# RWKV block inverse in 64x64 quarters of TensorE, interleaved pairs and heads, gated rows on two engines, and the block loop in another place

## The chip, the cores and the metric

The kernel runs on one core of one Trainium2 chip. The metric is the device time of one execution, in microseconds (us), as the median of several runs. A core has TensorE (PE; its weight loads are shown apart as PEld), VectorE (DVE), ScalarE (ACT), GpSimd (POOL) and SyncE (SP), which here only issues transfers; every engine works through its own instructions in order, and semaphores make one wait for another. DMA queues move data between the chip's large memory and the on-chip memory.

## What is computed

One decoder layer over 256 tokens of width 2048, in float32. The input is normalised and projected; 8 attention heads of 128 and 16 RWKV heads of 64 work on the projections beside each other; their outputs are projected back and added to the input. Then comes PEER, a retrieval over 128 x 128 experts of one neuron each, and a last normalisation.

```python
def rwkv7_time_mix(...):
    def step(state, inp):
        rt, wt, kt, vt, at, bt = inp
        sa = jnp.einsum('bhij,bhj->bhi', state, at)
        state = (state * wt[:, :, None, :] + sa[..., None] * bt[:, :, None, :]
                 + vt[..., :, None] * kt[..., None, :])
        y = jnp.einsum('bhij,bhj->bhi', state, rt)
        return state, y
...
def peer_ffn(x, wq, sub_keys, u, v):
    q = (xt @ wq).reshape(T, H, 2, PEER_HALF)
    s = jnp.einsum('thpc,hpnc->thpn', q, sub_keys).astype(jnp.float32)
    sv, si = lax.top_k(s, K)
    cand = (sv[:, :, 0, :, None] + sv[:, :, 1, None, :]).reshape(T, H, K * K)
    best, bi = lax.top_k(cand, K)
    ...
    expert = (i1 * PEER_NKEYS + i2).astype(jnp.int32)
    gates = jax.nn.softmax(best, axis=-1)
    def chunk(args):
        hpre = jnp.einsum('cd,chkd->chk', xc, u[ec]).astype(jnp.float32)
        act = (jax.nn.gelu(hpre, approximate=False) * gc).astype(x.dtype)
        return jnp.einsum('chk,chkd->cd', act, v[ec])
...
h = h + jnp.concatenate([attn, rw], axis=-1) @ w_out[l]
h = h + peer_ffn(rmsnorm(h, norm2_g[l]), peer_wq[l], peer_sub_keys[l], peer_u[l], peer_v[l])
return rmsnorm(h, final_g)
```

## The kernel before

Products of float32 precision are made of three passes: weights and inputs are split into a rounded high part and the rest (`whi`, `wlo`). `prefetch` (L191) loads half a block of weights by SP's queue, ACT writes `whi` (L204), DVE writes `wlo` (L205), and `gemm_half` (L213) multiplies (L218 to L220). The order in which weights are fetched is the list `halves`, which must be the order in which the loops consume them.

**Stage A, 0 to 541 us: input projections, RWKV and attention.** `products` (L639) runs the gemms of 8 RWKV pairs (two heads of 64 in the 128 rows) and then of 8 attention heads. After each pair or head a generator, `rwkv` (L376) or `attn` (L578), joins the list `live`; `step_all` advances up to four of them by one step between parts of gemms. In these generators the sequence is cut in NC = 4 chunks of CH = 64 tokens. A chunk needs the inverse of a triangular 64x64 matrix per head. It is built by doubling in five levels: `X` is the transpose of `XT` (L493), one group of four matmuls (one per chunk) gives `pw` (L496), DVE masks it into `wm` (L498), a second group gives `px` (L502), which DVE adds to `XT` (L504). Both heads of a pair stand in one 128x128 block-diagonal matrix, so that each matmul has 128 rows and 128 weight columns and 64 moving columns. The inverse is applied to a 128-wide right side after that. `clear` (L633) issues transfers that set the expert table `rows_d` in memory to zero, two for each pair and one for each head.

**541 to 736 us**: the output projection and PEER's queries.

**Stage D, 736 to 1568 us: the hidden stage.** `hidden` (L1125) goes over the 128 keys of u. A key takes 16 matmuls of 512 columns by `whi` (L240) and 16 of 256 by `wlo` (L242), from two halves of u, so two `wlo` splits of DVE. Then ACT and DVE sum the two parts (`part`, L1137 and L1138; the key's partial sum), and ACT writes the gelu into `A` (L1122), a ring of tiles of eight keys. Beside the keys three generators run, paced by shares of PE's time (`beside`): `both_choices` finds each token's experts (DVE), `tables` makes the table of gates by expert (DVE and POOL; marks, L937 and L939), then `places`, the row of each expert in a packed table; and `scatter` (L1098) takes a key's gelu, multiplies it by its gates into `at` (`gated`, L1080, the multiplication is L1093) and writes the rows of that key to their places in `rows_d` by an indirect DMA that POOL issues (L1107). `at` is a tile of seven keys' rows; the first key of a tile also copies the expert numbers into its last columns (`eint`, L1085). `gates_of` (L1072) loads the gates of eight keys. All of it is on POOL for the first 126 keys. The scheduler sets the place of each instruction on its engine from this program order and from its own estimate of when operands are ready.

**Stage E, 1568 to 2029 us: the values.** Blocks of 128 packed experts are read back, their rows of v gathered and multiplied into 8 accumulators (two token halves t, four columns each). Two lists of 28 blocks belong to one half only; 52 blocks are for both. A loop `For_i(MID, count)` behind them takes what stands beyond 52; `count` is computed, and here it is not above 52, so the loop makes no trip.

**Tail**: DVE adds the residual to the eight accumulators (`yr`, L1295), then the last norm and the output.

Of the kernel before, what the change touches and what calls it, by code (L numbers as in the profile page):

```python
# [10 lines left out]
F32 = mybir.dt.float32  # L11
# [57 lines left out]
def consts():  # L69
# [6 lines left out]
    c[:, K_MSK:K_MSK + P] = same & (p[:, None] < p[None])  # L76
# [3 lines left out]
    for i in range(6):  # L80
        n = 1 << i
        lv = (p[:, None] // (2 * n) == p[None] // (2 * n)) & (p[:, None] % (2 * n) >= n) & (p[None] % (2 * n) < n)
        c[:, K_LV + i * P:K_LV + (i + 1) * P] = lv
        if i == 0:
            c[:, K_M1T:K_M1T + P] = lv.T
# [69 lines left out]
def block_kernel(ctx: ExitStack, tc: tile.TileContext, x, cols, consts, w_lora, w_gate, w_rkv, w_qkv,  # L155
# [25 lines left out]
    for w, n in ((w_gate, 2), (w_rkv, 3 * RJ), (w_qkv, 3 * AH)):  # L181
        halves += [(w[m, i].rearrange("p k c -> p (k c)"), HK * P) for m in range(n) for i in range(2)]
# [163 lines left out]
    wms = [p1.tile([P, NC, P], F32, name=f"wm{i}") for i in range(1, 6)]  # L346
# [8 lines left out]
    mska = kc(K_MSK, 128).rearrange("p (h t) -> p h t", h=2).unsqueeze(1).to_broadcast([P, 2, 2, CH])  # L355
    mskr = kc(K_MSK + 128, 192).unsqueeze(1).to_broadcast([P, 2, 192])
# [3 lines left out]
    idb = ident.unsqueeze(1).to_broadcast([P, NC, 128])  # L360
# [15 lines left out]
    def rwkv(j, r, k, vv):  # L376
# [94 lines left out]
        XT = W("XT", [P, NC, 128], 2)  # L471
        lv = lambda i: kc(K_LV + i * 128, 128)
        nc.vector.tensor_tensor(XT, M[:, :, 0:128], kc(K_M1T, 128).unsqueeze(1).to_broadcast([P, NC, 128]),
# [10 lines left out]
        for i in range(1, 6):  # L484
            n = 1 << i
            nblk = P // (2 * n)
# [13 lines left out]
            px = bank("px", [P, NC, CH])  # L500
# [138 lines left out]
    def products():  # L639
# [18 lines left out]
        for j in range(RJ):  # L658
            while len(live) > 4:
                step_all()  # L660
# [13 lines left out]
        for h in range(AH):  # L674
            while len(live) > 4:
                step_all()
# [646 lines left out]
```

## Time and profile before

| | |
|---|---|
| median of 3 runs | 2046.03 us (2045.47 to 2049.38) |
| profiled execution | 2048.21 us, its span 2046.3 us |
| PE busy | 1935.7 us (95%) |
| DVE busy | 1437.7 us (70%) |
| ACT busy | 1062.9 us (52%) |
| POOL busy | 712.1 us (35%) |
| hidden stage | 736 to 1568 us of the span |
| value stage | 1600 to 2029 us, PE busy throughout |

The profile is one execution. A window of it gives how long each engine was busy in a stretch, the granted TensorE clock as a share of full speed, and what the DMA engines moved. A wait is put down to the instruction that came last. Where a mean of a line mixes shapes, the single rows are read.

### The profile page before, as it was taken

To read this page: it belongs to the slowest core of one execution; us is meant where nothing else is said; L and a number is where in the kernel's file an instruction comes from. 1 tells how busy PE (TensorE), PEld (TensorE's weight loads), DVE (VectorE), ACT (ScalarE), POOL (GpSimd) and SP (SyncE) were. 2 spreads that over 40 slices of the span, in tenths; PEclk is the share of its full clock that TensorE was granted. 3 is DMA by queue.
4 is the path that set the end of the run, shared out by engine and by line. 5 is a ranking of instruction groups with operands and counts; after the bars stand their busy time and mean duration, and the time that the engine had idled before them with its cause. 6 is when DMAs were issued, how large, how long until landed. Compare 5 with 4: busy or idle time off the path is not lost. (4 is left out here: it accounts for less than half of the span.)

```text
span 2046.3 us, 31447 instructions
## 1 busy us (share of the span) xinstructions
PE 1935.7 (95%) x11804; PEld 1723.3 (84%) x11804; DVE 1437.7 (70%) x2090; ACT 1062.9 (52%) x1696; POOL 712.1 (35%) x654
## 2 busy tenths in 40 slices
PE   7888999999999999999999999887998999999996
PEld 6788999999879998878888888776887788888885
DVE  6766878766556888999878866544755666666665
ACT  4534554345455444677676744433444555555554
POOL 7211211100000000023424269998986333333322
PEclk9999999999999999999999999998999999999998
DMA  8999322225576666556666678786888887878783
GB/s 248 258 247 246 98 87 87 88 83 146 190 227 198 184 180 188 173 175 197 215 195 217 196 237 264 248 267 229 270 267 271 343 284 280 296 286 293 281 297 141
DMA packets 135291, 443.91 MB, mean 217 GB/s; under 512 B 14369, under 2 KB 52257, under 8 KB 118497
## 3 DMA queue, kind: packets, MB, share of 16 engines
q1 hardware_dynamic: 106992, 289.24, 47.7%
q0 software_dynamic: 28144, 152.65, 20.4%
q8 instruction: 93, 1.52, 0.3%
q14 instruction: 62, 0.50, 0.1%
HBM read 380.07 MB, written 61.76 MB: 216 GB/s over the span
## 5 line engine op out<-in xcount | busy, mean ns | idle before, releaser
L205 DVE TENSOR_TENSOR wlo<-raw,whi 128x1024 fp32r<-128x1024 f32 (+1 forms) x408 | 569.6, 1402 | 301.1 <-ACT whi L204 291.9
L240 PE MATMUL ps_gm<-nx,whi 128*128 128x512 f32 x2048 | 731.8, 400 | 24.9 <-ACT whi L204 21.9
L204 ACT ACTIVATE whi<-raw 128x1024 fp32r<-128x1024 f32 (+1 forms) x408 | 429.5, 1055 | 384.2 <-issue 89.5
L242 PE MATMUL ps_gm<-nx,wlo 128*128 128x256 f32 x2048 | 579.4, 283 | 14.2 <-DVE wlo L205 14.2
L240 PEld LDWEIGHTS ps_gm<-nx,whi 128*128 128x128 f32 x2048 | 387.8, 189 | 112.6 <-ACT whi L204 22.6
L242 PEld LDWEIGHTS ps_gm<-nx,wlo 128*128 128x128 f32 x2048 | 390.3, 191 | 20.1 <-DVE wlo L205 19.7
L249 DVE TENSOR_TENSOR vlo<-vraw,vhi 128x2048 fp32r<-128x2048 f32 x108 | 247.9, 2297 | 151.6 <-ACT vhi L248 146.1
L248 ACT ACTIVATE vhi<-vraw 128x2048 fp32r<-128x2048 f32 x108 | 205.9, 1913 | 156.3 <-DVE vlo L249 146.8
L1205 POOL DMA_INDIRECT vraw<-in_v_dram,ag x108 | 145.1, 1343 | 294.8 <-PE ps_gm L1194 210.0
L218 PE MATMUL ps_gm<-xh,whi 128*128 128x256 f32 x640 | 192.7, 301 | 0.8 <-ACT whi L204 0.8
L220 PE MATMUL ps_gm<-xh,wlo 128*128 128x256 f32 x640 | 185.1, 289 | 3.2 <-DVE wlo L205 3.1
L219 PE MATMUL ps_gm<-xl,whi 128*128 128x256 f32 x640 | 185.6, 290 | 0.0
L1107 POOL DMA_INDIRECT rows_d<-at,place x126 | 169.5, 1345 | 36.9 <-POOL at L1093 15.8
L951 POOL TENSOR_TENSOR mt<-gc 128x1024 f32<-128x1024 f32 x16 | 39.7, 2482 | 345.5 <-ACT gc L979 345.5
L1122 ACT ACTIVATE A<-part 128x256 f32<-128x256 f32 x128 | 53.1, 415 | 166.7 <-DVE part L1138 131.3
L1093 POOL TENSOR_TENSOR at<-A,gt 128x256 f32<-128x256 f32 x126 | 129.2, 1041 | 5.4 <-DMA gt<-gate_d 3.6
L220 PEld LDWEIGHTS ps_gm<-xh,wlo 128*128 128x128 f32 x640 | 122.8, 192 | 4.6 <-DVE wlo L205 4.2
L218 PEld LDWEIGHTS ps_gm<-xh,whi 128*128 128x128 f32 x640 | 122.9, 192 | 1.9 <-ACT whi L204 1.2
L219 PEld LDWEIGHTS ps_gm<-xl,whi 128*128 128x128 f32 x640 | 122.9, 192 | 0.7
L807 POOL DMA_DIRECT2D skb<-in_sk_dram x16 | 8.6, 540 | 250.7 <-ACT mh L248 167.7
L945 ACT ACTIVATE ob<-ob,pick 128x128 f32<-128x128 f32 x256 | 83.9, 390 | 19.6 <-DVE ob L937 19.6
L373 POOL TENSOR_TENSOR df<-ext 128x256 f32<-128x256 f32 (+1 forms) x28 | 23.8, 850 | 155.3 <-DVE ext L371 142.4
(1521 smaller groups left out, 3925.5 us busy)
## 6 DMA issues: line engine op xcount, KB each, us to landing
raw<-in_u_dram SPq DMA_DIRECT2D x256, 512.0 KB, 4.1
raw<-in_w_rkv_dram SPq DMA_DIRECT2D x48, 512.0 KB, 7.3
raw<-in_w_qkv_dram SPq DMA_DIRECT2D x48, 512.0 KB, 3.6
rows_d<-zt SPq DMA_DIRECT2D x23, 1028.0 KB, 15.8
raw<-in_w_out_dram SPq DMA_DIRECT2D x32, 512.0 KB, 3.9
raw<-in_wq_dram SPq DMA_DIRECT2D x32, 512.0 KB, 3.6
gate_d<-gc SPq DMA_DIRECT2D x16, 1024.0 KB, 6.5
gt<-gate_d POOLq DMA_DIRECT2D x16, 1024.0 KB, 9.0
```

The lines of the kernel that those rows point to most:

```text
L204: nc.scalar.activation(hi[:, :n], raw[:, :n], AF.Copy)
L205: state["dve"] = nc.vector.tensor_tensor(lo[:, :n], raw[:, :n], hi[:, :n].bitcast(F32), op=ALU.subtract)
L218: nc.tensor.matmul(ps, a, xh(kt), start=first and k == 0, stop=False)
L219: nc.tensor.matmul(ps, a, xl(kt), start=False, stop=False)
L220: state["mm"] = nc.tensor.matmul(ps, b, xh(kt), start=False, stop=last and k == HK - 1)
L240: nc.tensor.matmul(ps.rearrange("p z t -> p (z t)"), hi[:, k * P:(k + 1) * P], x_.rearrange("p z t -> p (z t)"), start=i + k == 0, stop=Fa ...
L242: state["mm"] = nc.tensor.matmul(ps[:, 0, :], lo[:, k * P:(k + 1) * P], x_[:, 0, :], start=False, stop=i == 1 and k == HK - 1, skip_group_ ...
L248: nc.scalar.activation(hi, src, AF.Copy)
L249: nc.vector.tensor_tensor(lo, src, hi.bitcast(F32), op=ALU.subtract)
L1093: eng.tensor_tensor(at[:, 0:T].rearrange("p (q t) -> p q t", q=KT), As[i2 // 8][:, k, :].rearrange("p (q t) -> p q t", q=KT), g.rearrange( ...
L1107: s_ = nc.gpsimd.indirect_dma_start(out=rows_d, out_offset=bass.IndirectOffsetOnAxis(ap=place[:, i2:i2 + 1], axis=0), in_=at, in_offset=None)
L1205: nc.gpsimd.indirect_dma_start(out=raw, out_offset=None, in_=vf, in_offset=bass.IndirectOffsetOnAxis(ap=ag[:, T:ROW].bitcast(I32), axis=0))
```

## The change

*Compact inverse.* `XT`, `X` and the `wm` tiles hold only the two 64x64 diagonal blocks, one above the other, [P, NC, 64] instead of [P, NC, 128]. Each level's group of four matmuls of 128x128 weights and 64 moving columns becomes eight matmuls, each on one head: 64 rows, 64 weight columns, 32 moving columns, rows and outputs in the same half of the partitions. The two mask operations behind `pc` become one. After the last level the compact inverse is expanded to its block-diagonal form by one POOL operation (`bd(XB_, XT)`).

*Order.* RWKV pairs and attention heads alternate: pairs 0, 1, 2, head 0, pair 3, head 1, up to pair 7, head 5, head 6, head 7. The weight list follows. After the first head the splits use one pool of tiles, as they did before after the last pair.

*Hidden stage.* `tables` waits until both halves are chosen. Shares and paces of the generators change. The multiplication of a gated row is on VectorE for even keys and on POOL for odd ones; the copy of the expert numbers stays on POOL.

*The block loop* stands in the middle of the value stage (at k == 40), not behind it.

```diff
+    ORDER = [("r", 0), ("r", 1)] + [x for j in range(2, RJ) for x in (("r", j), ("a", j - 2))] + [("a", AH - 2), ("a", AH - 1)]
+    blocks_ = [(w_gate, m) for m in range(2)]
+    for what, n in ORDER:
+        blocks_ += [((w_rkv if what == "r" else w_qkv), 3 * n + i) for i in range(3)]
...
-    wms = [p1.tile([P, NC, P], F32, name=f"wm{i}") for i in range(1, 6)]
+    wms = [p1.tile([P, NC, CH], F32, name=f"wm{i}") for i in range(1, 6)]
...
+    both = [slice(0, 64), slice(64, 128)]
...
-            nc.vector.tensor_tensor(M[:, q:q + 2, 0:128].rearrange("p a (h t) -> p a h t", h=2),
-                                    pc2[:, :, 0:CH].unsqueeze(2).to_broadcast([P, 2, 2, CH]), mska, op=ALU.mult)
-            nc.vector.tensor_tensor(M[:, q:q + 2, 128:320], pc2[:, :, CH:], mskr, op=ALU.mult)
+            nc.vector.tensor_tensor(M[:, q:q + 2, 64:320], pc2, msk, op=ALU.mult)
...
-            X = W("X", [P, NC, 128], XB)
+            X = W("X", [P, NC, CH], XB)
             nc.vector.transpose(X.rearrange("p c s -> p (c s)"), XT.rearrange("p c s -> p (c s)"))
-            pw = bank("pw", [P, NC, CH])
+
+            pw = bank("pw", [P, NC, CH // 2])
             for c in range(NC):
-                nc.tensor.matmul(o4(pw)[:, c], M[:, c, 0:128], lo_(X)[:, c], start=(c == 0), stop=(c == NC - 1),
-                                 skip_group_check=True)
+                for hs in both:
+                    nc.tensor.matmul(o4(pw)[hs, c], M[hs, c, 64:128], lo_(X)[hs, c], start=True, stop=True,
+                                     skip_group_check=True)
...
-                nc.tensor.matmul(o4(px)[:, c], wm[:, c, :], hi_(XT)[:, c], start=(c == 0), stop=(c == NC - 1),
-                                 skip_group_check=True)
+                for hs in both:
+                    nc.tensor.matmul(o4(px)[hs, c], wm[hs, c, :], hi_(XT)[hs, c], start=True, stop=True,
+                                     skip_group_check=True)
...
+        XB_ = W("XB", [P, NC, 128], 2)
+        bd(XB_, XT)
...
-            nc.tensor.matmul(sa_p, XT[:, c, :], r0, start=True, stop=True)
+            nc.tensor.matmul(sa_p, XB_[:, c, :], r0, start=True, stop=True)
...
+        for k, (what, n) in enumerate(ORDER):
+            while len(live) > 4:
+                step_all()
+            if what == "a":
+                state["pools"] = [spl]
+            yield from (pair if what == "r" else head)(n)
...
-        while t not in chosen:
+        while 0 not in chosen or 1 not in chosen:
             yield 0
...
-            yield 1.5
+            yield 2.6
...
-            eng.tensor_copy(rows[0][:, 0:n * ROW].rearrange("p (n c) -> p n c", c=ROW)[:, :, T].bitcast(I32),
+            nc.gpsimd.tensor_copy(rows[0][:, 0:n * ROW].rearrange("p (n c) -> p n c", c=ROW)[:, :, T].bitcast(I32),
                                   eint[:, i2:i2 + n])
...
-            at = gated(i2)
+            at = gated(i2, nc.gpsimd if i2 % 2 else nc.vector)
...
-            yield 1.5
+            yield 2.3
...
-    beside = [[both_choices(), 0.55, 0.0], [tables(), 0.38, 0.0], [scatter(), 1.0, 0.0]]
+    beside = [[both_choices(), 0.6, 0.0], [tables(), 0.45, 0.0], [scatter(), 1.0, 0.0]]
...
+        if k == 40:
+
+            count = nc.values_load(nblk[0:1, 0:1], min_val=0, max_val=128,
+                                   skip_runtime_bounds_check_because="a count of at most 16384 experts in blocks of 128")
+            with tc.For_i(MID, count, 1) as i:
+                rows[2] = rows[1]
+                ag, _ = rows_at(i * P + BM)
+                rows[1] = rows[2]
+                block((0, 1), *divided(ag, gather(ag)), False)
```

How this moves instructions, at two places. Numbers behind a name tell buffers apart; `xN` is a run of alike instructions.

VectorE in the hidden stage, around the 82nd key, before: two splits of u and one partial sum for each key, and nothing else.

```order
L1138 TENSOR_TENSOR part_13604<-part_13604,ps_gm_13548 128x256
L205 TENSOR_TENSOR wlo_13670<-raw_13667,whi_13669 128x1024
L205 TENSOR_TENSOR wlo_13699<-raw_13696,whi_13698 128x1024
L1138 TENSOR_TENSOR part_13663<-part_13663,ps_gm_13607 128x256
L205 TENSOR_TENSOR wlo_13729<-raw_13726,whi_13728 128x1024
L205 TENSOR_TENSOR wlo_13756<-raw_13753,whi_13755 128x1024
L1138 TENSOR_TENSOR part_13722<-part_13722,ps_gm_13666 128x256
```

VectorE around the 82nd key now (L211 is the split, L1151 the partial sum, L1106 the multiplication of a gated row; `at_13919` holds the rows of keys 21 to 27, `at_14065` those of 28 to 34, `at_14222` the next seven):

```order
L1151 TENSOR_TENSOR part_13847<-part_13847,ps_gm_13793 128x256
L1106 TENSOR_TENSOR at_13919<-A2_9503,gt0_13651 128x256
L1106 TENSOR_TENSOR at_13919<-A3_9958,gt1_13833 128x256 x2
L211 TENSOR_TENSOR wlo_13907<-raw_13904,whi_13906 128x1024
L1106 TENSOR_TENSOR at_14065<-A3_9958,gt1_13833 128x256
L211 TENSOR_TENSOR wlo_13934<-raw_13931,whi_13933 128x1024
L1151 TENSOR_TENSOR part_13900<-part_13900,ps_gm_13850 128x256
...
L1106 TENSOR_TENSOR at_14065<-A4_10422,gt0_14000 128x256 x2
L211 TENSOR_TENSOR wlo_13989<-raw_13986,whi_13988 128x1024
L1151 TENSOR_TENSOR part_13957<-part_13957,ps_gm_13903 128x256
...
L1106 TENSOR_TENSOR at_14222<-A4_10422,gt0_14000 128x256 x2
```

The gated rows of even keys from 22 on stand among the splits of some three keys; the rows of keys 0 to 20 stand at keys 75 to 77, and none between.

POOL in its scatters before (L1093 the multiplication, L1107 the scatter, L1085 the copy of expert numbers, L1075 the load of gates): two rows are made, then two are scattered.

```order
L1093 TENSOR_TENSOR at_13247<-A2_9154,gt0_13178 128x256 x2
L1107 DMA rows_d_70<-at_13247,place_8196 39936x257 x2
L1085 COPY at_13355<-eint_8197 128x7
L1093 TENSOR_TENSOR at_13355<-A2_9154,gt0_13178 128x256 x2
L1107 DMA rows_d_70<-at_13355,place_8196 39936x257 x2
```

POOL in its scatters now (L1106, L1120, L1098 and L1088 are the same four), from the end of the tile `at_13761` of keys 14 to 20:

```order
L1106 TENSOR_TENSOR at_13761<-A2_9503,gt0_13651 128x256
L1120 DMA rows_d_70<-at_13761,place_8536 39936x257 x2
L1098 COPY at_13919<-eint_8537 128x7
L1106 TENSOR_TENSOR at_13919<-A2_9503,gt0_13651 128x256 x2
L1120 DMA rows_d_70<-at_13919,place_8536 39936x257 x4
L1088 DMA gt0_14000<-gate_d_69 128x16x128
L1106 TENSOR_TENSOR at_13919<-A3_9958,gt1_13833 128x256
L1120 DMA rows_d_70<-at_13919,place_8536 39936x257 x2
L1106 TENSOR_TENSOR at_13919<-A3_9958,gt1_13833 128x256
L1098 COPY at_14065<-eint_8537 128x7
```

One row is made for two scatters, and the copy into a new tile stands where it stood, behind the scatters of the tile before it; VectorE's rows of that tile wait for this copy.

## Rows read from the trace of the kernel before

**Rows 1.** The page: busy time, share of the span and instructions of each engine.

```profile
PE 1935.7 (95%) x11804; PEld 1723.3 (84%) x11804; DVE 1437.7 (70%) x2090; ACT 1062.9 (52%) x1696; POOL 712.1 (35%) x654
```

**Rows 2.** Windows: stretch, length, busy of each engine, granted clock, DMA share, GB/s.

```profile
100.00:150.00 50.00, 44.25 (x351) 43.62 (x350) 33.14 (x68) 21.14 (x34) 8.71 (x15) 0.93 1.07 251
200.00:541.00 341.00, 336.06 (x2702) 326.18 (x2701) 249.73 (x495) 159.64 (x302) 37.26 (x46) 1.00 0.35 104
...
1219.83:1568.20 348.37, 317.44 (x1770) 273.85 (x1768) 201.68 (x168) 147.95 (x221) 310.95 (x276) 0.96 0.79 256
...
2029.00:2046.00 17.00, 0.19 (x1) 0.00 (x0) 10.62 (x20) 8.42 (x22) 6.06 (x4) 0.61 0.33 124
```

**Rows 3.** Windows of line L1138 (partial sums) alone: DVE busy, clock, DMA.

```profile
736.00:1219.83 483.83, 29.52 (x72) 0.99 0.64 198
749.80:788.60 38.80, 2.90 (x7) 1.00 0.65 190
```

**Rows 4.** Waits from 1220 to 1568 us, and windows of all engines around one.

```profile
ACT A L1122 <- POOL at L1093: 30.7, 2, 21.8
PE ps_gm L240 <- ACT whi L204: 21.9, 2, 17.0
...
1370.00:1392.00 22.00, 4.97 (x29) 4.16 (x27) 0.80 (x3) 1.70 (x3) 19.64 (x23) 0.67 0.46 155
1392.00:1420.00 28.00, 27.54 (x144) 23.57 (x144) 16.31 (x15) 12.06 (x20) 23.94 (x23) 0.89 0.82 269
```

**Rows 5.** Lines L496 and L218 by form, L496's window after 200 us, and timeline.

```profile
L496 PEld LDWEIGHTS ps_pw<-X,M x320: 186/192/192, 96.7 to 431.3; 128*128 128x128 f32 x160
L218 PEld LDWEIGHTS ps_px<-xh,ml x8: 160/162/165, 13.5 to 16.9; 128*96 128x96 f32 x8
200.00:541.00 341.00, 30.84 (x240) 29.58 (x240) 1.00 0.35 104
232.33 0.97 PEld L496 LDWEIGHTS ps_pw<-X,M 128*128 128x128 f32 x8 [0.22 <-issue]
```

**Rows 6.** Line L493 on VectorE: times in ns, least, median, most.

```profile
L493 DVE STREAM_TRANSPOSE X<-XT x40: 685/702/714, 95.6 to 429.8; 128x512 f32<-128x512 f32 x40
```

**Rows 7.** POOL's timeline from 1235 us: start, length, instruction, idle before; and L1107.

```profile
1235.63 1.20 POOL L1075 DMA_DIRECT2D gt<-gate_d  x1
...
1241.99 0.96 POOL L1107 DMA_INDIRECT rows_d<-at,place  x1 [0.30 <-issue]
1242.97 1.81 POOL L1093 TENSOR_TENSOR at<-A,gt 128x256 f32<-128x256 f32 x2
1244.95 1.81 POOL L1107 DMA_INDIRECT rows_d<-at,place  x1 [0.16 <-POOL at L1093]
...
1249.80 0.21 POOL L1085 COPY at<-eint 128x7 int32<-128x7 int32 x1
...
L1107 POOL DMA_INDIRECT rows_d<-at,place x126: 961/1054/2045, 1219.8 to 1563.4; - x126
```

**Rows 8.** POOL's timeline from 1381 us, while the other engines stand still.

```profile
1381.02 1.66 POOL L1093 TENSOR_TENSOR at<-A,gt 128x256 f32<-128x256 f32 x2
1382.84 1.01 POOL L1107 DMA_INDIRECT rows_d<-at,place  x1 [0.17 <-POOL at L1093]
1384.15 0.97 POOL L1107 DMA_INDIRECT rows_d<-at,place  x1 [0.30 <-issue]
```

**Rows 9.** Window of all engines while the experts are chosen.

```profile
900.00:940.00 40.00, 33.87 (x210) 29.66 (x209) 40.00 (x45) 25.37 (x52) 16.56 (x10) 1.00 0.51 167
```

**Rows 10.** Timeline of the tail: the first final sum, and the seventh.

```profile
2029.58 0.69 DVE L1295 TENSOR_TENSOR yr<-yr,ps_mm 128x512 f32<-128x512 f32 x1 [7.86 <-PEq L1264]
...
2034.63 0.66 DVE L1295 TENSOR_TENSOR yr<-yr,ps_gm 128x512 f32<-128x512 f32 x1
```

**Rows 11.** POOL's timeline: the first and the seventh scatter, and what follows.

```profile
1219.83 2.04 POOL L1107 DMA_INDIRECT rows_d<-at,place  x1 [5.86 <-DVE place L1060]
...
1230.13 0.22 POOL L1085 COPY at<-eint 128x7 int32<-128x7 int32 x1
```

More of the change, by code (lines that the diff above doesn't have):

```diff
@@ L75, in consts @@
     same = p[:, None] // 64 == p[None] // 64
-    c[:, K_MSK:K_MSK + P] = same & (p[:, None] < p[None])
+    c[:, K_MSK + 64:K_MSK + P] = (p[:, None] % 64) < np.arange(64)[None]
     c[:, K_MSK + P:K_MSK + 192] = (p[:, None] % 64) <= np.arange(64)[None]
@@ L81, in consts @@
         n = 1 << i
-        lv = (p[:, None] // (2 * n) == p[None] // (2 * n)) & (p[:, None] % (2 * n) >= n) & (p[None] % (2 * n) < n)
-        c[:, K_LV + i * P:K_LV + (i + 1) * P] = lv
+        r, t = p[:, None] % 64, np.arange(64)[None]
+        lv = lambda a, b: (a // (2 * n) == b // (2 * n)) & (a % (2 * n) >= n) & (b % (2 * n) < n)
+        c[:, K_LV + i * 64:K_LV + (i + 1) * 64] = lv(r, t)
         if i == 0:
-            c[:, K_M1T:K_M1T + P] = lv.T
+            c[:, K_M1T:K_M1T + 64] = lv(t, r)
+            c[:, K_M1T + 64:K_M1T + 128] = r == t
     c[:, K_HM:K_HM + P] = (p[:, None] // 64 == np.arange(P)[None] // 64)
@@ L180, in block_kernel @@
         halves += [(w_lora[m, i].rearrange("p k c -> p (k c)"), HK * LOR) for m in range(2)]
-    for w, n in ((w_gate, 2), (w_rkv, 3 * RJ), (w_qkv, 3 * AH)):
-        halves += [(w[m, i].rearrange("p k c -> p (k c)"), HK * P) for m in range(n) for i in range(2)]
+    ORDER = [("r", 0), ("r", 1)] + [x for j in range(2, RJ) for x in (("r", j), ("a", j - 2))] + [("a", AH - 2), ("a", AH - 1)]
+    blocks_ = [(w_gate, m) for m in range(2)]
+    for what, n in ORDER:
+        blocks_ += [((w_rkv if what == "r" else w_qkv), 3 * n + i) for i in range(3)]
+    halves += [(w[m, i].rearrange("p k c -> p (k c)"), HK * P) for w, m in blocks_ for i in range(2)]
     KP = (4, 5, 6, 7, 0, 1, 2, 3)
@@ L359, in block_kernel @@
     hm2 = lambda t: t.unsqueeze(1).to_broadcast([P, 2, CH])
-    idb = ident.unsqueeze(1).to_broadcast([P, NC, 128])
+    idb = kc(K_M1T + 64, 64).unsqueeze(1).to_broadcast([P, NC, CH])
+    both = [slice(0, 64), slice(64, 128)]
     def bd(dst, src):
@@ L465, in rwkv @@
             pc2 = pc.rearrange("p (c i) n -> p c (i n)", c=2)
-            nc.vector.tensor_tensor(M[:, q:q + 2, 0:128].rearrange("p a (h t) -> p a h t", h=2),
-                                    pc2[:, :, 0:CH].unsqueeze(2).to_broadcast([P, 2, 2, CH]), mska, op=ALU.mult)
-            nc.vector.tensor_tensor(M[:, q:q + 2, 128:320], pc2[:, :, CH:], mskr, op=ALU.mult)
+            nc.vector.tensor_tensor(M[:, q:q + 2, 64:320], pc2, msk, op=ALU.mult)
             yield
-        XT = W("XT", [P, NC, 128], 2)
-        lv = lambda i: kc(K_LV + i * 128, 128)
-        nc.vector.tensor_tensor(XT, M[:, :, 0:128], kc(K_M1T, 128).unsqueeze(1).to_broadcast([P, NC, 128]),
+        XT = W("XT", [P, NC, CH], 2)
+        lv = lambda i: kc(K_LV + i * 64, 64)
+        nc.vector.tensor_tensor(XT, M[:, :, 64:128], kc(K_M1T, 64).unsqueeze(1).to_broadcast([P, NC, CH]),
                                 op=ALU.mult)
@@ L485, in rwkv @@
             n = 1 << i
-            nblk = P // (2 * n)
+            nblk = CH // (2 * n)
             lo_ = lambda t: t.rearrange("p c (b z i) -> p c b z i", z=2, i=n)[:, :, :, 0, :]
@@ L657, in products, with pair @@
         state["pools"] = [spl, spl, spare[0]]
-        for j in range(RJ):
-            while len(live) > 4:
-                step_all()
+        def pair(j):
             got = []
@@ L672, in products, with head @@
             clear(2)
-        state["pools"] = [spl]
-        for h in range(AH):
-            while len(live) > 4:
-                step_all()
+        def head(h):
             got = []
@@ L1260, in block_kernel @@
                 block((t,), *cut[j], ends[t] == j)
-    count = nc.values_load(nblk[0:1, 0:1], min_val=0, max_val=128,
-                           skip_runtime_bounds_check_because="a count of at most 16384 experts in blocks of 128")
-    with tc.For_i(MID, count, 1) as i:
-        ag, _ = rows_at(i * P + BM)
-        block((0, 1), *divided(ag, gather(ag)), True)
+        if k == 40:
[6 more added lines that the diff above has]
+                block((0, 1), *divided(ag, gather(ag)), False)
     gf = mp.tile([P, D], F32, tag="ml", name="gf")
```

5 lines of the change are left out of this document (2 added, 3 removed).

## The prediction

> **What bounds the kernel now.** The profiled execution took 2048.2 us, 2.2 us above the median of the runs; its span is 2046.3 us. I sum against 2048.2 and take 2.2 off at the end. TensorE (PE) is busy for 95% of the span [rows 1], so I read the windows by stage next, to see where the other 5% lies and what else could become late [rows 2].
>
> Up to 200 us the DMA engines are full (share 1.07) while PE has gaps (44.25 of 50 us): zeros for the expert table and the weights share the queues, and a PE saving there is hidden. From 200 to 541 us PE is busy for 336.06 of 341: there the path is PE's sum of work. The hidden stage (keys of u, 736 to 1568 us) has its gaps in its second part: after the first scatter at 1219.83 PE is busy for 317.44 of 348.37 us. The tail from 2029 us has no PE work at all [rows 2].
>
> A key of u takes 5.55 us where nothing disturbs it (7 keys in 38.8 us, [rows 3]). 72 keys have their partial sum before the first scatter [rows 3]; by the times of the sums on either side it falls at key 72.4. The other 55.6 keys would take 308.6 us and take 348.4: 40 us of excess. The waits show most of it: the gelu (ACT, A, L1122) waited twice for POOL's gated rows (`at`, L1093), 30.7 us in all, and PE waited 21.9 us behind it [rows 4]. After the longer of these gaps the granted clock is 0.89 for 28 us, a loss of 3.1 us [rows 4]; with as much for the other I put the two stalls at 28 us, and 12 us are spread over the keys. The stalls are POOL being late: it makes each gated row and scatters it, about 2.7 us for each of 126 (1219.8 to 1563.4, [rows 7]), and the ring of A tiles is only released by POOL's reads.
>
> **The change part by part.**
>
> *Compact inverse.* A level of the RWKV inverse costs two groups of four matmuls, each two records; one group holds PE for 0.97 us, 0.121 us a record [rows 5]. There are 80 groups; 60 lie behind 200 us (240 of the 320 records of L496, and as many of L502), the others under the full DMA. Now a group has 16 records of half the weight columns and half the moving columns. The trace shows no 64x64 matmul, so I bound it. If a record costs by its columns (0.06 us), the group stays at 0.97: nothing. If two quarters run side by side, 0.49 us: 60 x 0.48 = 29 us less. If a record keeps its 0.121 us, 1.94 us: 58 us more. If PE empties at each change of shape and pays the gap of 0.22 us seen ahead of one group [rows 5] twice a group: 26 us more. I take nothing: the nearest row is the weight load of 96 columns, 162 ns against 192 for 128 [rows 5], a cost that falls with columns. The Trainium skill, "TensorEngine Tiling (Array Packing)", section Key Properties, says that a change of tiling mode drains TensorE, which speaks against this change, and that different tiles can load and multiply in parallel, which speaks for it; no run here has shown either. By the first the sum would be 26 us higher, by the second alone 29 us lower.
>
> VectorE's transposes (L493, 702 ns, forty of them [rows 6]) halve, and the mask operations become fewer. VectorE is off the path there; PE's idle time from 200 to 541 us is 5 us in all [rows 2], and I give 2 us of that back. POOL gets one more expansion per pair; it is busy for 37 of 341 us [rows 2], which hides it. If that cover were gone it would delay only the state steps of its own pair.
>
> *RWKV and attention interleaved.* The same gemms, records and zeros, and the weight order follows the loop. The zeros sit at the same places of SyncE's order, so the first 200 us stay. Before, RWKV is done early and the last heads are nearly pure gemms; now the last RWKV pair and three heads stand at the end, and some of their chain falls between the first matmuls of the output projection. I put 3 us on that, with 0 and 8 as ends: it is a wait of a few steps of some 1 us each.
>
> *Gated rows split between VectorE and POOL.* POOL loses half of its multiplications, and the ring of A tiles is released earlier: key 99 now needs scatter 37, not 63, so the two stalls go, 28 us. But what is late next? In the order of the changed program VectorE's gated row for a new `at` tile waits for POOL's copy of the expert numbers into that tile, and this copy stands in POOL's order behind nearly all scatters of the tile before. VectorE's gated rows do not stand one by one: they stand in six bunches, at keys 75 to 77, 82 to 85, 90 to 92, 98 to 101, 106 to 109 and 114 to 115. Within a bunch the waits reach from scatter 0 to 13, 21 to 35, 42 to 55, 63 to 77, 84 to 97 and 105 to 111: 73 scatters against 14 keys. POOL cannot run ahead between bunches, since scatter 22 (42, 64 and so on) needs VectorE's row 22. Behind a gated row that waits stand the splits of u (wlo), which PE needs for its next key, and the partial sums, which ACT needs: so PE stops. VectorE is ahead of PE by no more than the half key that its split serves, 2.77 us; I allow 2.5 us a bunch.
>
> What does POOL take for a scatter now? For two scatters: one own row, a scatter behind it, and one that follows at once. With VectorE at work [rows 7]: 0.91 (half of 1.81) + 0.16 + 1.81 + 0.30 + 0.96 = 4.14 us, 2.07 a scatter; a load of gates for each eight (1.20) and a copy for each seven (0.21) add 0.18: 2.25 us. With VectorE idle (0.80 us busy in 22, [rows 4]) the same steps take [rows 8] 0.83 + 0.17 + 1.01 + 0.30 + 0.97 = 3.28, so 1.64 + 0.18 = 1.82 us. The Trainium skill, "SBUF — State Buffer", section "SBUF: two separate sides", says that VectorE and GpSimd share a port pair as an exclusive lock; the trace agrees (1.81 against 1.01 us for the same scatter). By that rule alone, with the 63 new VectorE rows on the port too, 2.25 would hold throughout, and the time would be about 2096 us.
>
> PE's idle time is then 73 x c - 14 x 5.55 - 6 x 2.5 = 73c - 92.7: 71.6 us at 2.25, 40.2 us at 1.82. In a bunch POOL works about half of the time beside a busy VectorE and half beside a held one; I take the middle, 56 us. Five of the six gaps are about 10 us, and a long gap cost 3.1 us of clock: 12 us more in all at 2.5 each. The excess behind the first scatter becomes 12 + 56 + 12, less 3 us for the spread excess of the 14 keys that the bunches already cover: 77 us, against 40. So **plus 37 us** in the hidden stage, with ends of 20 and 53.
>
> *Tables held until both choices are done, other rates and paces.* VectorE is full at 900 to 940 us [rows 9]; the choices end some four keys earlier and the tables begin later, but the same VectorE work stands against the same keys: zero. The first scatter moves from key 72.4 to about 74.6; the keys in between only change sides.
>
> *The loop in the middle.* The loop runs zero times. At its old place it held VectorE until 2029.58, though t=0's sums were ready; the sums from there to the seventh, at 2034.63, follow one after the other [rows 10]. In the new order three of t=0's sums stand ahead of the last splits, so some 5 us of the tail go under PE's last matmuls. At its new place every engine, PE among them, stops at a count that must be loaded. The trace shows no such stop in mid-stream: it lies between nothing and the 5 us between those rows; I take 2 us, nearer to nothing, since the values and expert rows of the next blocks are already fetched. Net **minus 3 us**.
>
> Sum: 2048.2 - 2 + 3 + 37 - 3 = 2083, less 2.2: **2081 us**.
>
> **Rivals.**
> 1. *POOL is quick enough* (faster). If POOL's scatters go as the first seven did, 10.30 us for seven with all operands made, 1.47 each [rows 11], the idle time is 73 x 1.47 - 92.7 = 15 us with 4 us of clock; the excess is 31 instead of 40, and the time 2046 - 2 + 3 - 9 - 3 = 2035 us. For it: the seven show that POOL can go at that pace when nothing has to be made. Against it: half of the scatters still stand behind an own multiplication. The point from which it decides is c = 1.57 us, where hidden-stage gain and loss cancel; the quick stretch already shows 1.82.
> 2. *Quarters side by side.* 29 us off the stage from 200 to 541 us, the rest as forecast: 2052 us. Its ground is that two halves of PE would then serve two heads at once; the trace has no row in which two matmuls run side by side.
> 3. *Quarters cost more*, by emptied PE at each change (2107 us) or by an unchanged price per record (2139 us). For it: a weight load falls by only 16% for a quarter fewer columns [rows 5], so part of a record's time does not fall with columns.
> 4. *The interleaving does nothing* is part of the forecast: PE's sum does not change.
>
> **How the numbers follow.** Forecast (PE stops behind VectorE's bunches, 2060 to 2097 us): 0.52. Rival 1: 0.24. Rival 2: 0.12, split evenly over faster, same and slower, since D's ends of 20 and 53 move it from 2035 to 2068. Rival 3: 0.12. A difference below 0.2%, 4.1 us, can hardly be told from none. Faster: 0.24 + 0.04 + 0.01 for a faster forecast case = 0.29; same 0.07; slower 0.64. The range reaches from 2022 us (rival 1 with some overlap of quarters) to 2105 us (the forecast's top with a small price for quarters); about 0.1 is left out on either side.
>
> **What would show it.** Right: VectorE's gated rows wait for POOL by 5 to 18 us in bursts near keys 76, 84, 91, 100 and 108, with PE gaps there and the granted clock low behind them; POOL's scatters wait for VectorE between bursts; ACT waits for `at` no more; the tail is about 5 us shorter. Wrong: the waits of VectorE on POOL are a few us in all, or PE has no gaps after the first scatter; or a group of quarter matmuls takes half or double of 0.97 us; or the output projection starts more than 10 us later.

## The result and the profile after

The changed kernel took 2064.27 us (2062.07 to 2069.72, 4 runs) beside 2045.85 us: a ratio of 1.009, 95% interval 1.0067 to 1.0113. Run again later beside other kernels (e11 below) it was at 1.0115 (1.0095 to 1.0134). It is slower by about 1%, as forecast in sign and by half in size (2081 us was forecast, a ratio of 1.017). The profiled execution was the slowest of the four, 2069.7 us with a span of 2068.0.

The page of the changed kernel: busy time of each engine, then the slices of PE, POOL and the granted clock.

```profile
PE 1940.7 (94%) x12444; PEld 1709.5 (83%) x12444; DVE 1412.6 (68%) x2136; ACT 1067.7 (52%) x1702; POOL 650.0 (31%) x600
...
PE   7898999999999999999999878877899999999998
...
POOL 7211111110000000014443447677653333333332
PEclk9999999999999999999999999988999999999999
```

PE works as long as before [rows 1], POOL 62 us less, and the total is longer: the loss is time in which PE waits, above all in the slices from 23 to 29, the second part of the hidden stage. Windows of the changed kernel (stretch, length, busy of each engine, clock, DMA share, GB/s), to be read against [rows 2]:

```profile
100.00:150.00 50.00, 47.71 (x532) 44.35 (x529) 34.65 (x77) 21.88 (x36) 8.33 (x14) 0.97 1.09 265
200.00:523.00 323.00, 317.28 (x3099) 297.44 (x3099) 227.63 (x477) 163.90 (x302) 44.64 (x57) 0.99 0.34 110
1219.49:1600.00 380.51, 321.29 (x1706) 274.85 (x1704) 195.79 (x222) 142.50 (x212) 248.88 (x221) 0.92 0.71 229
```

The first gemm of the queries marks where the first stages end. These rows of the line of that gemm give least, median and most duration in ns, and the first and last start; before first, changed second.

```profile
L218 PE MATMUL ps_gm<-yh,whi x256: 277/283/365, 635.5 to 735.5; 128*128 128x256 f32 x128
```

```profile
L224 PE MATMUL ps_gm<-yh,whi x256: 277/283/365, 619.6 to 719.7; 128*128 128x256 f32 x128
```

So three stretches differ between the two profiles. **Up to the queries: 15.9 us less** (635.5 to 619.6). **Hidden stage: 48 us more** (832 to 880 us), from the last start of the queries' gemm (735.5 and 719.7) to the last start of a product by `whi` of u, in the last key (1567.7 and 1599.6). **From there to the end: 10 us less** (478.6 to 468.4). The sum, 22 us, is the difference of the spans.

Where the hidden stage loses, the waits from 1219.4 to 1600 us of the changed kernel tell (total, times, longest):

```profile
POOL rows_d L1120 <- DVE at L1106: 70.3, 12, 21.2
DVE at L1106 <- POOL at L1098: 69.1, 10, 15.3
```

and over the stretch from 1200 us on, those of PE:

```profile
PE ps_gm L246 <- DVE part L1151: 32.0, 9, 13.2
...
PE ps_gm L248 <- DVE wlo L211: 27.2, 9, 7.9
```

ACT's two waits for POOL (30.7 us, [rows 4]) are gone. In their place VectorE waits for POOL's copy of expert numbers 69 us, POOL waits for VectorE's rows 70 us, and PE stands behind VectorE for 59 us. From the first scatter on PE stands still for 59 us in all, against 31 before: 22 behind ACT [rows 4] and 9 behind VectorE, in these rows of the kernel before:

```profile
PE ps_gm L242 <- DVE wlo L205: 6.0, 9, 1.1
...
PE ps_gm L240 <- DVE part L1138: 2.9, 2, 1.6
```

PE is also busy for longer on each key: 321.29 us for 53.6 keys, 5.99 each, against 317.44 for 55.6, 5.71 each, at a mean granted clock of 0.92 against 0.96 [rows 2]. That is 15 us more, and 43 us with the 28 us of standing still: what the hidden stage loses behind the first scatter.

One bunch in full, the one at keys 90 to 92. VectorE's timeline (start, length, instruction, idle before):

```profile
1334.82 0.67 DVE L1106 TENSOR_TENSOR at<-A,gt 128x256 f32<-128x256 f32 x1
...
1346.14 0.44 DVE L1151 TENSOR_TENSOR part<-part,ps_gm 128x256 f32<-128x256 f32 x1
1348.02 1.22 DVE L211 TENSOR_TENSOR wlo<-raw,whi 128x1024 fp32r<-128x1024 f32 x1 [1.43 <-ACT whi L210]
1364.53 1.15 DVE L1106 TENSOR_TENSOR at<-A,gt 128x256 f32<-128x256 f32 x2 [15.28 <-POOL at L1098]
1365.60 1.21 DVE L211 TENSOR_TENSOR wlo<-raw,whi 128x1024 fp32r<-128x1024 f32 x1
1366.73 0.41 DVE L1151 TENSOR_TENSOR part<-part,ps_gm 128x256 f32<-128x256 f32 x1
```

POOL's timeline beside it:

```profile
1336.30 1.04 POOL L1120 DMA_INDIRECT rows_d<-at,place  x1 [15.50 <-issue]
...
1356.86 0.86 POOL L1106 TENSOR_TENSOR at<-A,gt 128x256 f32<-128x256 f32 x1
1357.89 1.00 POOL L1120 DMA_INDIRECT rows_d<-at,place  x1 [0.17 <-issue]
1359.20 0.96 POOL L1120 DMA_INDIRECT rows_d<-at,place  x1 [0.30 <-issue]
...
1364.29 0.21 POOL L1098 COPY at<-eint 128x7 int32<-128x7 int32 x1
```

And PE's:

```profile
1353.70 0.28 PE L248 MATMUL ps_gm<-nx,wlo 128*128 128x256 f32 x1
1367.19 0.79 PE L246 MATMUL ps_gm<-nx,whi 128*128 128x512 f32 x1 [13.21 <-DVE part L1151]
```

Ahead of the bunch POOL had stood for 15.50 us. Its line names no releaser; by the order it waited for VectorE's gated row, which was made at 1335.49 us, 0.8 us ahead of the scatter. Then VectorE reaches a row of a new tile at 1349 us; POOL still has scatters to issue, at 3.33 us for two (1356.86 to 1360.19), and makes the copy at 1364.29. VectorE's partial sum, queued behind, is made at 1366.73, and PE, which needs its bank of sums, starts again at 1367.19. Each engine waits in turn for what the other has queued late.

In the first stage, the form of a group of quarter matmuls in the changed kernel, and then PE's timeline around one group before and one in the changed kernel: the matmul ahead of it, the group, and two matmuls behind it.

```profile
L502 PEld LDWEIGHTS ps_pw<-X,M x640: 129/135/227, 96.7 to 491.0; 64*64 64x64 f32 x160
```

```profile
215.15 0.28 PE L220 MATMUL ps_gm<-xh,ml 128*128 128x256 f32 x1
215.27 1.00 PE L502 MATMUL ps_px<-XT,wm 128*128 128x64 f32 x8
216.08 0.36 PE L218 MATMUL ps_gm<-xh,ml 128*128 128x256 f32 x1
216.28 0.28 PE L219 MATMUL ps_gm<-xl,ml 128*128 128x256 f32 x1
```

```profile
205.48 0.28 PE L226 MATMUL ps_gm<-xh,wlo 128*128 128x256 f32 x1
205.69 0.66 PE L509 MATMUL ps_px<-XT,wm 64*64 64x32 f32 x16
206.27 0.38 PE L224 MATMUL ps_gm<-xh,whi 128*128 128x256 f32 x1
206.49 0.28 PE L225 MATMUL ps_gm<-xl,whi 128*128 128x256 f32 x1
```

From the first record of such a group to the next matmul's start PE is held for 0.585 us (median of the 77 groups that the trace has whole); the groups before took 0.813 us by the same count. 0.228 us for each of 80 groups would be 18 us. But PE also loses time where the shape changes: from the matmul ahead to the group's first record it is 0.209 us, against 0.119 before, and from the matmul behind the group to the one after it 0.222, against 0.202 (medians of the same groups). From the matmul ahead to the second one behind it is 1.131 us before and 1.016 now, so 0.115 us a group is left, 9.2 us for 80 groups.

### The profile page after: what moved, and what is told of

It reads as the page before. It is cut to its first block, busy times and chain, and to the rows that moved or that the text cites. A ratio compares the mean times of both kernels' runs of the same rounds, so it can differ in the third digit from the quotient of the medians.

```text
span 2068.0 us, 32694 instructions
## 1 busy us (share of the span) xinstructions
PE 1940.7 (94%) x12444; PEld 1709.5 (83%) x12444; DVE 1412.6 (68%) x2136; ACT 1067.7 (52%) x1702; POOL 650.0 (31%) x600
## 5 line engine op out<-in xcount | busy, mean ns | idle before, releaser
L211 DVE TENSOR_TENSOR wlo<-raw,whi 128x1024 fp32r<-128x1024 f32 (+1 forms) x418 | 531.3, 1275 | 269.5 <-ACT whi L210 268.9
L1218 POOL DMA_INDIRECT vraw<-in_v_dram,ag x108 | 149.1, 1381 | 293.9 <-PE ps_gm L1207 200.9
L224 PE MATMUL ps_gm<-xh,whi 128*128 128x256 f32 x720 | 222.3, 309 | 1.7 <-ACT whi L210 1.7
L226 PE MATMUL ps_gm<-xh,wlo 128*128 128x256 f32 x720 | 208.0, 289 | 3.3 <-DVE wlo L211 2.5
L225 PE MATMUL ps_gm<-xl,whi 128*128 128x256 f32 x720 | 208.7, 290 | 0.0
L1120 POOL DMA_INDIRECT rows_d<-at,place x126 | 166.7, 1323 | 131.6 <-DVE at L1106 70.3
L226 PEld LDWEIGHTS ps_gm<-xh,wlo 128*128 128x128 f32 x720 | 139.8, 194 | 5.6 <-DVE wlo L211 4.3
L224 PEld LDWEIGHTS ps_gm<-xh,whi 128*128 128x128 f32 x720 | 139.5, 194 | 5.1 <-ACT whi L210 2.3
L225 PEld LDWEIGHTS ps_gm<-xl,whi 128*128 128x128 f32 x720 | 140.1, 195 | 0.9
L1106 DVE TENSOR_TENSOR at<-A,gt 128x256 f32<-128x256 f32 x65 | 46.8, 757 | 79.3 <-POOL at L1098 69.1
L950 DVE TENSOR_TENSOR ob<-iota,pick 128x512 f32<-128x512 f32 x64 | 72.7, 1136 | 3.2 <-POOL act L970 3.1
L224 PE MATMUL ps_gm<-yh,whi 128*128 128x256 f32 x256 | 73.5, 288 | 0.0
```

The costliest lines, as they stand in the source:

```text
L211: state["dve"] = nc.vector.tensor_tensor(lo[:, :n], raw[:, :n], hi[:, :n].bitcast(F32), op=ALU.subtract)
L224: nc.tensor.matmul(ps, a, xh(kt), start=first and k == 0, stop=False)
L225: nc.tensor.matmul(ps, a, xl(kt), start=False, stop=False)
L226: state["mm"] = nc.tensor.matmul(ps, b, xh(kt), start=False, stop=last and k == HK - 1)
L1120: s_ = nc.gpsimd.indirect_dma_start(out=rows_d, out_offset=bass.IndirectOffsetOnAxis(ap=place[:, i2:i2 + 1], axis=0), in_=at, in_offset=None)
L1218: nc.gpsimd.indirect_dma_start(out=raw, out_offset=None, in_=vf, in_offset=bass.IndirectOffsetOnAxis(ap=ag[:, T:ROW].bitcast(I32), axis=0))
```

## The experiments

The theory after the comparison: the quarters make the first stage shorter, the mutual waits of VectorE and POOL make the hidden stage longer, and the block loop's place makes the tail shorter. Ratios are to runs of the kernel before on the same chip; two ratios that are set against each other can come from different chips.

**e1: the inverse alone.** The kernel before with the compact inverse; order, hidden stage and loop as before.

```diff
-                nc.tensor.matmul(o4(pw)[:, c], M[:, c, 0:128], lo_(X)[:, c], start=(c == 0), stop=(c == NC - 1),
+                for hs in both:
+                    nc.tensor.matmul(o4(pw)[hs, c], M[hs, c, 64:128], lo_(X)[hs, c], start=True, stop=True,
```

> The kernel before with the compact inverse alone. Theory A (the quarters themselves are cheaper on PE: in the trace of the changed kernel a group of 16 records holds PE for 0.585 us against 0.812 us for the 8 records before, 80 groups): 18 us less than before, some of it lost under the full DMA of the first 200 us, so 2028 to 2034 us. Rival (the gain of the first stage comes from the interleaving of pairs and heads): within 4 us of 2046.

Measured: 0.9954 (0.9939 to 0.997), 9 us less. The queries begin at 627.4 us, 8 us earlier:

```profile
L220 PE MATMUL ps_gm<-yh,whi x256: 278/283/365, 627.4 to 727.5; 128*128 128x256 f32 x128
```

The group takes 0.585 us here too, and the matmul ahead of it starts 0.209 us earlier, as in the changed kernel. So PE's rows give 9.2 us, which is what the time shows. Theory A had the sign and was twice too large, because it counted from the group's first record and left out what PE loses at the changes of shape.

**e2: the interleaving alone.**

```diff
-        for j in range(RJ):
+        for k, (what, n) in enumerate(ORDER):
```

> The kernel before with pairs and heads interleaved (and the weights in that order), nothing else. Theory A: PE's sum is the same, the first stage ends within 4 us of where it did, 2043 to 2050 us. Rival (interleaving fills PE's waits in the state steps): the output projection begins 10 to 18 us earlier, 2028 to 2036 us.

Measured: 0.9985 (0.9969 to 1.0002), no clear difference. The queries begin at 636.2 us, against 635.5 before.

```profile
L222 PE MATMUL ps_gm<-yh,whi x256: 278/283/365, 636.2 to 736.2; 128*128 128x256 f32 x128
```

The interleaving by itself gives nothing.

**e8: the changed kernel with the full inverse.**

```diff
-            pw = bank("pw", [P, NC, CH // 2])
+            pw = bank("pw", [P, NC, CH])
```

(and with it all of the inverse as before.)

> The changed kernel with the inverse as before, in 128x128 matmuls. Theory A (quarters save 0.227 us for each of 80 groups, and with the pairs spread over the stage only the first 200 us hide some): 14 to 18 us slower than the changed kernel, PE's last input gemm ends at about 536 us. Rival (interleaving saves part of it): 8 us slower or less.

Measured: 1.0166 (1.014 to 1.0191) against 1.009 and 1.0115 of the changed kernel on two chips: 10 to 16 us slower. The queries begin at 635.7 us again:

```profile
L222 PE MATMUL ps_gm<-yh,whi x256: 277/283/365, 635.7 to 735.7; 128*128 128x256 f32 x128
```

So the time reaches the lower part of theory A's 14 to 18 us, or falls below it. In the first profile of the changed kernel the mark was 619.6, 16 us earlier. But nine profiles have both the quarters and the interleaving (the changed kernel, its repeat, e3 to e7, e9 and e10), and there it lies between 619.6 and 626.8 us, with 624.1 in the middle. So the quarters are worth 9 to 16 us with pairs and heads interleaved, 12 in the middle, and 8 without, in the one profile of e1. With this scatter it is not shown that the order matters for what the quarters save.

**e3: the hidden stage as before**, all else changed.

```diff
-            at = gated(i2, nc.gpsimd if i2 % 2 else nc.vector)
+            at = gated(i2)
...
-            yield 2.3
+            yield 1.5
...
-    beside = [[both_choices(), 0.6, 0.0], [tables(), 0.45, 0.0], [scatter(), 1.0, 0.0]]
+    beside = [[both_choices(), 0.55, 0.0], [tables(), 0.38, 0.0], [scatter(), 1.0, 0.0]]
```

> The changed kernel with the hidden stage of before (all gated rows on POOL, the old shares and paces, tables each after its own choice). Theory A (the hidden stage alone loses time, 46 to 48 us in the profiles): 2064 - 47 = 2017 us, ACT waits for POOL's gated rows about 30 us again, VectorE does not wait for POOL. Rival (part of the loss is a later effect of the earlier, faster first stage): 2030 us or more.

Measured: 0.9905 (0.9871 to 0.9939), about 38 to 43 us under the changed kernel by the difference of the ratios. The expectation was 46 to 48, and the time, 2032 us beside 2051, is 10 us above it. But by the marks of the first section the hidden stage lasts 831 us in this trace, as long as before (832), so its loss is gone in full. What is missing lies elsewhere: the queries begin at 624.7, not 619.6, and the stretch behind the last key is 478 us, as before, though the loop stands in the middle. The two waits of ACT are back as they were:

```profile
ACT A L1135 <- POOL at L1106: 30.4, 2, 22.0
...
PE ps_gm L246 <- ACT whi L210: 22.0, 2, 17.0
```

So the loss is in the hidden stage.

**e6: the split alone undone**, the new shares and paces kept.

```diff
-            at = gated(i2, nc.gpsimd if i2 % 2 else nc.vector)
+            at = gated(i2)
...
-            nc.gpsimd.tensor_copy(rows[0][:, 0:n * ROW]
+            eng.tensor_copy(rows[0][:, 0:n * ROW]
```

> The changed kernel with the split of gated rows undone, everything else, the new shares and paces too, as changed. Theory A (the split makes the loss): VectorE waits for POOL no more, the two stalls of ACT on gated rows return in some size, time 30 to 45 us below the changed kernel's, ratio to before 0.988 to 0.996. Rival (the later and slower tables and the pace of 2.3 make it): ratio above 1.002.

Measured: 0.9971 (0.9959 to 0.9983). Undoing the split alone gains 24 to 30 us of the loss. The hidden stage is even shorter than before, 813 us by the same marks. The stalls of ACT did not return, against what I expected, and why they did not is not settled; another wait came in their place, at the end. POOL's last scatter is issued at 1569.53 us, 30 us behind the last key (1539.6), and the blocks wait for it (POOL's timeline, then the waits):

```profile
1569.53 1.00 POOL L1120 DMA_INDIRECT rows_d<-at,place  x1 [0.28 <-POOL at L1106]
...
ACT ah L254 <- DMA ag<-rows_d: 19.2, 1, 19.2
```

That is 13 us more time than in e3. POOL is not slower here: from the first scatter to the last it takes 348.0 us, against 346.0 in e3. But its first scatter is issued at 1221.5 us, against 1211.3 there: the queries end 2 us later, and up to the first scatter the new shares and paces take 8 us more. So the last scatter is later too, while the keys behind the first scatter last only 318 us. POOL did need relief, then; the question is what the relief waits for.

**e4: one of POOL's steps moved.** The split stays; VectorE makes the copy itself.

```diff
-            nc.gpsimd.tensor_copy(rows[0][:, 0:n * ROW]
+            nc.vector.tensor_copy(rows[0][:, 0:n * ROW]
```

> The changed kernel with one line moved: the copy of the expert numbers into a new tile of gated rows is made by VectorE, not by POOL; the multiplications stay split. Theory A (VectorE waits for that copy behind POOL's scatters, 69 us in 10 waits): VectorE now waits only for scatters two to three tiles further back, at most a few us a bunch, PE's gaps behind the first scatter shrink from some 63 us to 15 (10 to 25) and the time falls by 40 to 55 us, to 2009 to 2025 us. Rival (VectorE is late because the split rows themselves are too much for it, or POOL is the bound either way): 2055 us or more.

Measured: 1.0113 (1.0082 to 1.0143). No gain at all: the expectation missed by 50 us. The waits from 1200 to 1610 us show why:

```profile
DVE at L1106 <- DMA gt<-gate_d: 71.1, 7, 15.9
POOL rows_d L1120 <- DVE at L1106: 67.1, 7, 23.8
```

VectorE waits as long as before, now for the load of gates. That load is issued by POOL too and stands in its order behind scatters as the copy does. I had seen both in the order and reckoned with one.

**e9: the other step moved.** The gates are loaded by SyncE's queue, the copy stays on POOL.

```diff
-            nc.gpsimd.dma_start(gts[g], gate_d[:, :, g * P:(g + 1) * P])
+            nc.sync.dma_start(gts[g], gate_d[:, :, g * P:(g + 1) * P])
```

> The changed kernel with the gates loaded by SyncE's queue, the copy of expert numbers still on POOL. Theory A (either step of POOL's queue is enough to hold VectorE; taking out the copy alone left the time as it was): VectorE waits for POOL's copy as in the changed kernel, 50 to 70 us, ratio to before 1.004 to 1.012. Rival (the load of gates alone was the binding step, and the copy's wait was only covering it): ratio 0.985 to 0.993, as with both taken out.

Measured: 1.0101 (1.0077 to 1.0125), no gain either:

```profile
DVE at L1106 <- POOL at L1098: 59.5, 8, 16.2
```

**e5: both steps moved**, the edits of e4 and e9 together.

```diff
-            nc.gpsimd.tensor_copy(rows[0][:, 0:n * ROW]
+            nc.vector.tensor_copy(rows[0][:, 0:n * ROW]
...
-            nc.gpsimd.dma_start(gts[g], gate_d[:, :, g * P:(g + 1) * P])
+            nc.sync.dma_start(gts[g], gate_d[:, :, g * P:(g + 1) * P])
```

> The changed kernel with both of POOL's steps that VectorE waits for taken out of POOL's queue: the copy of expert numbers is made by VectorE and the gates are loaded by SyncE's queue. With the copy alone moved, VectorE's waits went over to the load of gates (71 us in 7 waits, issued from POOL's queue behind scatters). Theory A (the loss is VectorE's place behind POOL's queue, by whichever step): PE's gaps behind the first scatter fall below 25 us, the excess of keys 72 to 127 from 85 to about 40, the time 40 to 50 us below the changed kernel's, ratio to before 0.985 to 0.992. Rival (POOL's rate of some 2.2 us a scatter against bunches is the bound, whichever queue the steps stand in; or the load now holds SyncE's u transfers): the time stays within 15 us of the changed kernel's, ratio 1.002 or more.

Measured: 0.9876 (0.9858 to 0.9893), 44 to 49 us under the changed kernel by the ratios. The profiled execution took 2010.8 us; the other four took 2023.1 to 2032.3, so the rows below stand for the best case. The same waits, from 1190 to 1570 us:

```profile
DVE at L1106 <- DMA gt<-gate_d: 12.8, 9, 3.3
POOL rows_d L1120 <- DVE at L1106: 12.5, 8, 3.6
PEld ps_gm L246 <- DVE part L1151: 10.3, 9, 3.1
PEld ps_gm L248 <- DVE wlo L211: 8.7, 12, 1.2
```

By the marks, the hidden stage lasts 823 us, against 880 in the changed kernel and 832 before. The split is what it was, VectorE's gated rows stand in the same bunches (at keys 74 to 76, 81 to 83, 88 to 91 and so on), and POOL's issue of a scatter is no cheaper: its median is 1.30 us, against 1.01 in the changed kernel. Only what VectorE waits for stands no longer in POOL's queue, and the loss is gone. That settles the cause: either step suffices to hold VectorE, and both must go.

**e7: the loop back at the end.**

```diff
-        if k == 40:
...
+    count = nc.values_load(nblk[0:1, 0:1], min_val=0, max_val=128,
```

> The changed kernel with the block loop back behind the last block. Theory A (the loop's end held VectorE's final sums; in the profiles the part from PE's last matmul to the end went from 17.1 to 9.2 us): 5 to 8 us slower than the changed kernel. Rival (the stop in the middle of the value stage costs as much as it saves): within 2 us of it.

Measured: 1.0151 (1.0127 to 1.0176), 7 to 12 us slower than the changed kernel by the ratios, which come from different chips. The trace shows a part of it: from PE's last matmul to the end it is 16.1 us, against 9.2 in the changed kernel, while the stop in the middle (1.94 us) is saved. That is a net of 5 us. VectorE's first final sum waits for the loop again, behind PE's last matmul, while in the changed kernel it stands 8 us ahead of it. First e7, then the changed kernel:

```profile
2058.63 0.69 DVE L1308 TENSOR_TENSOR yr<-yr,ps_mm 128x512 f32<-128x512 f32 x1 [7.86 <-PEq L1277]
```

```profile
2050.36 0.68 DVE L1311 TENSOR_TENSOR yr<-yr,ps_mm 128x512 f32<-128x512 f32 x1
...
2058.43 0.39 PE L1207 MATMUL ps_gm<-vhi,al__19655 128*128 128x512 f32 x1
```

**e10: both steps moved, with the shares and paces of before.** The edits of e5, and:

```diff
-            yield 2.3
+            yield 1.5
...
-    beside = [[both_choices(), 0.6, 0.0], [tables(), 0.45, 0.0], [scatter(), 1.0, 0.0]]
+    beside = [[both_choices(), 0.55, 0.0], [tables(), 0.38, 0.0], [scatter(), 1.0, 0.0]]
```

(also the places' 2.6 back to 1.5, and each table after its own choice.)

> The changed kernel with copy and gates out of POOL's queue, and the shares and paces of before (choices 0.55, tables 0.38, each table after its own choice, places and scatters 1.5). Theory A (the sum of VectorE's work on choices and tables is the same, 68 and 69 us of excess between keys 20 and 66 either way; an earlier start of the scatters gives POOL more room): within 6 us of the version with both taken out, on the faster side, ratio 0.983 to 0.989. Rival (a pace of 1.5 packs VectorE's gated rows closer, so that VectorE waits for POOL's landings again): 10 us or more slower than it.

Measured: 0.9831 (0.9814 to 0.9847), 2015.2 us beside 2051.1. This version beats both kernels, by 1.7% and 2.8%. It is 9 us faster than e5 by the ratios, a little more than the 6 us expected; but the two ran on different chips, and e5's own times spread over 21 us.

**e11: the changed kernel again**, beside e9 and e10.

> The changed kernel itself again, beside the two others on the same chip, as their yardstick. Expected ratio to before 1.007 to 1.012; the first stage ends 10 to 16 us earlier than before's, the hidden stage lasts 45 to 50 us longer.

Measured: 1.0115 (1.0095 to 1.0134). Its first stage ended 11 us earlier than in the profile of before (queries from 624.2 us), and its hidden stage lasted 879 us, 47 more. Over all traces, the hidden stage lasts 828 to 832 us where it is as before (e1 to e3 and the kernel before), 876 to 883 us with the split and one or both of the steps in POOL's queue (e4, e7, e8, e9, e11 and the changed kernel), and 821 to 823 with both taken out (e5 and e10).

## Why the prediction was right, and where its terms were off

- **The sign came from the right step.** The bunches, the waits of VectorE behind POOL's copy and the reverse waits of POOL are in the trace as read from the order. PE's idle time behind VectorE was put at 56 us (40.2 to 71.6); the two waits of PE sum to 59, of which some 9 stood there before the change. The excess behind the first scatter was put at 77 us; the stretch of 380.5 us with 53.6 keys of 5.55 us (297.5) has 83. The first scatter was put at key 74.6 and came there, the two stalls of ACT went. The rise in the hidden stage was put at 37 us with ends of 20 and 53; it was 48 in the profiles, of which 43 behind the first scatter and 3 to 5 ahead of it, where I had taken zero for the new shares and paces.
- **How near the sum came is partly luck.** Between the two profiles the hidden stage is 11 us worse than put, the first stage 17 us better (16 less, where 1 more was put), and the end 7 us better. These errors work against each other; 35 us more was forecast, 22 came in the profiles and 18 in the medians.
- **What the step named was incomplete.** I counted VectorE's wait on the copy. e4 and e9 show two steps of POOL's queue, each enough. The sum did not suffer, since the two waits lie on each other.
- **POOL's price.** While VectorE was held, two scatters took 3.33 us (3.28 reckoned). Rival 1 (1.47 us a scatter) is refuted by that row.
- **The quarters were mis-sized.** The term was zero, between 29 us less and 58 us more. PE's rows give 9.2 us less, e1 and e8 put the worth at 9 and 10 to 16 us. The step that failed was the choice "cost falls with columns, so twice the records at half the columns are even". A group went from 0.813 to 0.585 us, so a record takes 0.037 us, about a third of a record before (0.102). The price for emptying PE at each change of shape, put at 26 us, is in the rows too, but small: 0.09 us ahead of a group and 0.02 behind it, 9 us in all. The starts of the records hint at the ground of rival 2, two quarters side by side: they come in twos, 0.007 us apart, and 0.058 us from two to two. Which two they are is not shown. Rival 2 had the sign, but its 29 us are about three times what PE's rows give.
- **Also 0.97 us a group was too much**: I took the span of the records' loads, which overlaps with the neighbours. From the group's start to the next matmul's start it is 0.813. And the transposes of half the size did not halve: 0.445 us against 0.702. VectorE is off the path there.
- **The loop.** Net minus 3 us was put; the stretch behind the last key lost 10 us in the first profile and 7 in that of e11, and e7 gives 5 by its trace and 7 to 12 by the ratios. The price of its new place was right: PE stands for 1.94 us there (1773.69 to 1775.63 us), against 2. The gain in the tail was under-sized, 8 us (17.1 to 9.2) where 5 were put: not only the first three sums but the norm of t=0 and the start of its output now lie ahead of PE's end.
- **The interleaving** was put at plus 3 us and is nothing by e2.

## What to carry to other kernels

When work is dealt out from a late engine to an idle one, list every instruction that the receiving engine must wait for and see in whose queue each stands: if the helper's operands (a copy, a load that is merely issued there) queue on the engine that is being relieved, both run in lockstep, and whatever stands behind the wait, here the splits that feed TensorE, pays. Moving one such operand shows nothing while a second one stands in the same queue; the gain comes with the last. And a price for an instruction form that no row shows is better bounded by start-to-start times than by the durations of overlapped records; and these must reach from the instruction ahead of the new form to the second one behind it, or what is lost at the change is left out.

## What the hardware showed that I had not expected

A group of 16 records of quarter matmuls, 64 rows and 64 weight columns with 32 moving ones, takes 0.585 us, against 0.813 for 8 records of 128x128 with 64 moving columns, though the number of records doubles. Half of that gain is lost at the changes of shape: PE's start is 0.09 us later ahead of such a group than ahead of a full one, and 0.02 us is lost behind it. From the matmul ahead to the second one behind, the gain is 10% (1.131 to 1.016 us).

An indirect DMA's issue on POOL took 0.96 to 1.04 us in each of the 43 cases in which VectorE did nothing meanwhile; in the other 83 its median was 1.31 us and its longest 4.66 (trace of the changed kernel). The multiplication on POOL, 0.86 us with VectorE held, once took 5.29 us, while VectorE ran multiplications and splits back to back. POOL's row first, then VectorE's:

```profile
1341.76 5.29 POOL L1106 TENSOR_TENSOR at<-A,gt 128x256 f32<-128x256 f32 x1
```

```profile
1340.91 2.47 DVE L1106 TENSOR_TENSOR at<-A,gt 128x256 f32<-128x256 f32 x4
1343.27 1.25 DVE L211 TENSOR_TENSOR wlo<-raw,whi 128x1024 fp32r<-128x1024 f32 x1
1344.40 0.72 DVE L1106 TENSOR_TENSOR at<-A,gt 128x256 f32<-128x256 f32 x1
1345.01 1.25 DVE L211 TENSOR_TENSOR wlo<-raw,whi 128x1024 fp32r<-128x1024 f32 x1
```
